# Moving splits, squares, sums and a state scan from GpSimd to VectorE, in a list-scheduled decoder layer

## The chip, the core and the metric

The kernel runs on one core of a Trainium2 chip. A core has TensorE (PE in the profile: matmuls, with PEld for its weight loads), VectorE (DVE), ScalarE (ACT), GpSimd (POOL) and SyncE (SP), which here issues the DMAs. Each engine runs its own instructions in order; semaphores tie the engines together. The metric is the time of one execution in microseconds, lower is better.

## The reference

One inference step of a one-layer hybrid decoder, in float32, for 512 prompt tokens and 64 sample tokens (8 sequences of 8). All branches read one input projection of the normed input:

```python
z = rmsnorm(x, norm_g) @ w_in          # 2048 -> 3904 columns, split into u, gates, cq, ckv, kr, qm
y_ssm = ssm_mixer(u, h0)               # 32 groups, 64 complex states: x_t = a * x_(t-1) + b u_t, GELU, GLU
y_mla = attend(q(cq), k(ckv, kr), v(ckv))   # 8 heads; the sample also attends to 1024 paged past tokens
y_mem = softmax(rmsnorm(qm) @ mk.T) @ mv    # 4 heads, 256 memory tokens
o = concat(rmsnorm(y_g) * silu(gate_g) for g in (ssm, mla, mem))
y = x + o @ w_out
```

The outputs are y for both kinds of tokens, the new latent rows, the memory's keys and values, and the last SSM states.

## The kernel before

Tokens lie along the free dimension (576 columns, done as two halves of 288), features along the 128 partitions. To keep float32 accuracy with the faster fp32r matmuls, every operand is split into two 12-bit parts: `hi` (a rounded copy, by ScalarE or VectorE) and `lo` (`tensor_tensor` subtract: what rounding left). A product is then three matmuls (`mm3`): hi by hi, hi by lo, lo by hi. So nearly each tile that TensorE reads has gone through one `hi` and one `lo`: weights (`wunit`, 512 columns), activations (`split`, 576 columns), softmax results.

The code doesn't issue instructions directly. `Hymba.record` writes them down in a sequential order, part by part: x (input and its squares), params (the SSM's discretised parameters, 16-wide steps), u, e (the SSM's input tables), q, kv, kr, qm (first projections), memkv, scan, memq and memh (memory attention), mla, ssm, glu, mems and samp (the sample's attention), gates, fin (norms of the branches) and out. Each recorded instruction has one or more forms: an engine with the time that `Eng.time` gives for it. `Plan.arrange` gives each a place and a due time from `ROWS`. `Plan.schedule` then is a list scheduler: it steps through time, and gives each free engine the ready instruction that is due first; an engine may take an instruction that is meant for another, if that other would be later by `self.steal` (0.2272 us). What comes out is one fixed order for each engine. `Plan.emit` issues it, so that nearly all instructions have line 603 of the kernel (transposes L602, memsets L600).

Before the change GpSimd is one of the engines in that game. `lo` (line 708) is meant for VectorE and may be taken by GpSimd; squares in `act` (733) are meant for ScalarE and may be taken by either; sums by `gtt` (803: sums of squares, rotary combinations) are meant for GpSimd and may be taken by VectorE. The scan over the states, `ssm_scan` (1084), is 248 instructions on GpSimd: for each of 7 steps inside groups of 8 chunks, 2 sample steps, 15 steps over groups and 7 steps that carry these back, it does eight products and sums, 256, 128, 16 and 240 columns wide, on the state tiles Z (named t_672 and t_690 in the order of before, t_650 and t_676 in the order of the change) and small tiles (F). The tables that `padded` makes (1002, part e and part ssm) and the memsets are on GpSimd too. In the scheduler's prices the engines don't disturb each other.

Of the kernel before, what the change touches and what calls it, by code (L numbers as in the profile page):

```python
# [11 lines left out]
F32R = mybir.dt.float32r  # L12
# [6 lines left out]
P = 128  # L19
NT = 576          # 512 prompt tokens, then 64 sample tokens (sequence, step)  # L20
# [4 lines left out]
SIZES = [74, 3170, 1400]         # SBUF: slots, columns for small float32 tiles and float32r ones  # L25
# [3 lines left out]
NC = 144          # chunks of 4 tokens  # L29
ZW = 153          # 1 + 128 prompt chunk states, 8 x 3 sample ones  # L30

# columns of the packed vectors
# [3 lines left out]
# the order of the program's parts: rows of streams that run side by side, each with its share of the row  # L36
# [17 lines left out]
# in_proj tiles  # L54
T_U, T_CQ, T_CKV, T_KR, T_QM, T_GS, T_GM, T_GMEM = 0, 4, 8, 10, 11, 15, 19, 27
# columns of the packed constants
# [3 lines left out]
def host_consts():  # L60
# [9 lines left out]
    # sums of all rows, of each 32 rows, of all rows eight times: a window of 40 columns puts them where they belong  # L70
# [93 lines left out]
class Tile_:  # L164
    """a piece of SBUF or PSUM, placed when the plan is made"""
# [9 lines left out]
class View:  # L175
    """an access pattern on a tile that has no place yet"""
# [62 lines left out]
def latency(a, b):  # L239
    """from the end of an engine's work to the start of another's that needs it"""  # L240
    if a == b:
        return (0.0, 0.127, 0.02, 0.102, 0.1)[a]
    return 0.26 if b == PE else 0.2 if a == PE else 0.15


FREED = (0.2, 0.15, 0.15, 0.15, 0.1)    # from the end of a tile's last use to its next use, in SBUF


# spaces: SBUF's slots of 576 columns; tiles with a place of their own; arenas for small float32 and float32r tiles; PSUM; DRAM
SLOT, OWN, SMALL, SMALLR, BANKS, DRAM = range(6)  # L250
PITCH = 4096        # of a row of a tile that has no place yet


class Plan:
    """Records the kernel's instructions in a sequential order, then issues them in one that keeps the engines busy."""

    def __init__(self, F, R, PS, sizes, place):
# [7 lines left out]
        self.soon = 21.0755                     # when work is due that the tensor engine doesn't wait for  # L265
        self.edf = True
        self.margin = [0, 0, 730, 0, 0]
        self.steal = 0.2272                     # how much later an engine must be for another to take its work
        self.look, self.stall, self.tol = 12, 120.4994, 5.0000
        self.late = False                    # work that may wait until it is needed  # L270
        self.slack = 1.0                     # how long work may wait that frees memory
        self.window = [43.3422, 40.6910, 40.6910, 40.6910, 40.0202]

# [1791 lines left out]
```

## Time and profile before

| what | value |
|---|---|
| median of 3 runs | 1306.81 us (1303.35 to 1307.94) |
| span of the profiled execution | 1303.6 us |
| PE busy | 1205.4 us (92%) |
| DVE busy | 933.3 us (72%) |
| ACT busy | 540.8 us (41%) |
| POOL busy | 543.3 us (42%), 703 instructions |
| mean granted TensorE clock | 0.963 |

The page gives no other time for the profiled execution than its span. "Busy" is the time in which an engine has an instruction in hand; an instruction that stands still in the middle counts as busy. The clock is the share of TensorE's full speed that was granted: 1.0 is 2.4 GHz, 0.5 is 1.2 GHz.

### The profile page before, as it was taken

To read this page: it belongs to the slowest core of one execution; us is meant where nothing else is said; L and a number is where in the kernel's file an instruction comes from. 1 tells how busy PE (TensorE), PEld (TensorE's weight loads), DVE (VectorE), ACT (ScalarE), POOL (GpSimd) and SP (SyncE) were. 2 spreads that over 40 slices of the span, in tenths; PEclk is the share of its full clock that TensorE was granted. 3 is DMA by queue.
4 is the path that set the end of the run, shared out by engine and by line. 5 is a ranking of instruction groups with operands and counts; after the bars stand their busy time and mean duration, and the time that the engine had idled before them with its cause. 6 is when DMAs were issued, how large, how long until landed. Compare 5 with 4: busy or idle time off the path is not lost. (4 is left out here: it accounts for less than half of the span.)

```text
span 1303.6 us, 24011 instructions
## 1 busy us (share of the span) xinstructions
PE 1205.4 (92%) x8428; PEld 1130.6 (87%) x8428; DVE 933.3 (72%) x2007; ACT 540.8 (41%) x1238; POOL 543.3 (42%) x703
## 2 busy tenths in 40 slices
PE   7889987978689989899999999999999997999998
PEld 7789977978578788789899999999999887999998
DVE  8996799946899798997885757475766899622210
ACT  7222322333486477775564434343333354212100
POOL 5575289989888677782230101000001345100000
PEclk8889998989799899989999999999999989999999
DMA  8243342132021245533543424333333465434310
GB/s 293 93 124 116 120 145 67 41 128 67 19 80 54 63 111 188 181 119 94 162 142 111 132 90 128 96 108 108 126 118 94 135 214 163 160 103 150 116 63 28
DMA packets 93324, 151.53 MB, mean 116 GB/s; under 512 B 10803, under 2 KB 36787, under 8 KB 93203
## 3 DMA queue, kind: packets, MB, share of 16 engines
q1 hardware_dynamic: 93202, 150.00, 36.6%
q8 instruction: 66, 1.08, 0.3%
q14 instruction: 56, 0.45, 0.1%
HBM read 129.87 MB, written 17.73 MB: 113 GB/s over the span
## 5 line engine op out<-in xcount | busy, mean ns | idle before, releaser
L603 PE MATMUL PS<-t,t 128*128 128x288 f32 (+7 forms) x7976 | 1162.8, 303 | 46.7 <-DVE t L603 26.0
L603 PEld LDWEIGHTS PS<-t,t 128*128 128x128 f32 (+2 forms) x7976 | 1087.8, 190 | 102.1 <-DVE t L603 28.1
L603 ACT ACTIVATE t<-t 128x512 fp32r<-128x512 f32 (+6 forms) x484 | 288.0, 614 | 393.6 <-DVE t L603 117.7
L603 DVE TENSOR_TENSOR t<-t,t 128x512 fp32r<-128x512 f32 (+6 forms) x412 | 330.0, 815 | 105.1 <-ACT t L603 52.3
L603 POOL TENSOR_TENSOR t<-t,t 128x512 fp32r<-128x512 f32 (+6 forms) x160 | 229.5, 1442 | 339.4 <-PE PS L603 105.3
L603 ACT ACTIVATE t<-PS 128x256 f32<-128x256 f32 (+6 forms) x316 | 124.7, 425 | 174.4 <-PE PS L603 149.3
L603 DVE TENSOR_TENSOR t<-PS,t 128x288 f32<-128x288 f32 (+5 forms) x226 | 89.9, 426 | 102.8 <-PE PS L603 96.5
L603 DVE TENSOR_REDUCE F<-t 128x4 f32<-128x512 f32 (+1 forms) x137 | 94.9, 705 | 68.2 <-ACT t L603 67.1
L603 POOL TENSOR_TENSOR F<-t,F 128x256 f32<-128x256 f32 (+3 forms) x157 | 106.2, 695 | 12.1 <-DVE F L603 5.7
L603 DVE SCALAR_TENSOR_TENSOR t<-t,F,t 128x576 fp32r<-128x576 f32 (+5 forms) x84 | 77.7, 939 | 10.2 <-DMA t<-re 9.5
L603 ACT ACTIVATE t<-t,F 128x576 fp32r<-128x576 f32 (+6 forms) x93 | 60.0, 664 | 29.8 <-DVE t L603 11.5
L603 DVE TENSOR_SCALAR t<-t 128x512 fp32r<-128x512 f32 (+6 forms) x109 | 53.2, 492 | 20.8 <-PE PS L603 5.7
L600 POOL MEMSET t<- 128x4 f32 (+3 forms) x86 | 31.2, 373 | 83.6 <-PE PS L603 36.6
L603 ACT COPY t<-PS 128x64 f32<-128x64 f32 (+7 forms) x135 | 38.0, 299 | 66.5 <-PE PS L603 61.3
L603 DVE SCALAR_TENSOR_TENSOR t<-t,t 128x576 f32<-128x576 f32 (+1 forms) x68 | 62.0, 923 | 2.1 <-ACT t L603 1.9
L603 PE MATMUL PS<-t,R 128*40 128x384 f32 (+6 forms) x134 | 31.3, 332 | 32.9 <-ACT t L603 16.5
L603 DVE SCALAR_TENSOR_TENSOR F<-F 128x64 f32<-128x64 f32 (+5 forms) x157 | 57.9, 374 | 1.8 <-POOL F L603 0.4
L603 PEld LDWEIGHTS PS<-t,R 128*40 128x40 f32 (+3 forms) x134 | 17.3, 146 | 39.2 <-ACT t L603 17.4
L603 POOL TENSOR_TENSOR t<-t,F 128x16 f32<-128x16 f32 (+4 forms) x64 | 45.8, 715 | 4.2
L603 POOL TENSOR_TENSOR F<-F 128x16 f32<-128x16 f32 (+4 forms) x66 | 41.3, 626 | 8.0 <-DVE F L603 3.7
L603 POOL TENSOR_TENSOR R<-F,R 64x64 fp32r<-64x64 f32 (+1 forms) x8 | 4.5, 561 | 78.8 <-DVE R L603 62.1
L603 DVE TENSOR_TENSOR F<-F 128x16 f32<-128x16 f32 (+4 forms) x125 | 33.7, 287 | 1.0
(76 smaller groups left out, 493.8 us busy)
## 6 DMA issues: line engine op xcount, KB each, us to landing
t<-in_w_in SPq DMA_DIRECT2D x124, 256.0 KB, 3.1
t<-in_w_out SPq DMA_DIRECT2D x64, 256.0 KB, 3.7
t<-in_pages SPq DMA_DIRECT2D x64, 224.0 KB, 2.8
t<-in_xT SPq DMA_DIRECT2D x48, 288.0 KB, 4.7
t<-re SPq DMA_DIRECT2D x32, 256.0 KB, 3.1
t<-in_pages SPq DMA_DIRECT2D x64, 128.0 KB, 2.1
re<-t SPq DMA_DIRECT2D x24, 256.0 KB, 2.5
out_yT<-t SPq DMA_DIRECT2D x16, 288.0 KB, 2.1
```

The lines of the kernel that those rows point to most:

```text
L600: return real(r["out"], r["value"])
L603: return real(**r)
```

## The change

1. Forms are taken away: `lo` has no GpSimd form, squares have none, and `gtt` is recorded for VectorE alone. The scan is recorded for VectorE.
2. The scheduler gets a resource, `port`. `Eng.shared` says which forms take it: on GpSimd each instruction with an SBUF input; on VectorE each with two SBUF inputs, and copies and tensor_scalar from SBUF to SBUF. Such a form is not started before `port`, and sets `port` to its end less 0.07 us.
3. TensorE's prices in `time` and `weights` rise: 2.23 instead of 2.4 columns a nanosecond for products, 2.35 for weights.

`ROWS`, the window, `steal` and all other settings stay. Comments are removed, which moves the lines (603 becomes 614). The core of the diff:

```diff
+        self.early = 0.07
...
+        port = 0.0
...
+                if e in (DVE, POOL) and port > now + 1e-9 and not h:
+                    continue
...
+                    if op.forms[e][2] and port > now + 1e-9:
+                        skipped.append(item)
+                        tries += 1
+                        why = "port"
+                        continue
...
+                    if op.forms[e][2]:
+                        port = op.end - self.early
...
-            nxt = [a for a in avail if a > now + 1e-9]
+            nxt = [a for a in avail + [port] if a > now + 1e-9]
...
-        return fn, self.time(name, kw)
+        return fn, self.time(name, kw), self.shared(name, kw)
+
+    def shared(self, name, kw):
+        src = [kw[k] for k in ("in_", "in0", "in1") if isinstance(kw.get(k), View)]
+        n = sum(v.t.space != BANKS for v in src)
+        if self.eng == POOL:
+            return n > 0
+        return self.eng == DVE and (n > 1 or n == 1 and name in ("tensor_copy", "tensor_scalar") and kw["out"].t.space != BANKS)
...
-            return 2 * kw["in_"].shape[0] / 2.4e3
-        return size(kw["lhsT"]) * (2 if kw["lhsT"].dtype == F32R else 4) / 2.4e3
+            return 2 * kw["in_"].shape[0] / 2.35e3
+        return size(kw["lhsT"]) * (2 if kw["lhsT"].dtype == F32R else 4) / 2.35e3
...
-                return 0.003 + 2 * kw["in_"].shape[0] / 2.4e3
+                return 0.003 + 2 * kw["in_"].shape[0] / 2.23e3
...
-            return (k if kw["lhsT"].dtype == F32R else 4 * max(k, 64)) / 2.4e3 + 0.003
+            return (k if kw["lhsT"].dtype == F32R else 4 * max(k, 64)) / 2.23e3 + 0.003
...
-            o = [] if self.onpsum(in_) or not self.flex else [(self.G, "tensor_tensor", kw)]
-            self.V.record("tensor_tensor", (), kw, o)
+            self.V.record("tensor_tensor", (), kw)
...
-            o += [(e, "tensor_tensor", k_) for e in (self.V, self.G)]
+            o.append((self.V, "tensor_tensor", k_))
...
-        kw = dict(out=out, in0=a, in1=b, op=op)
-        self.G.record("tensor_tensor", (), kw, [(self.V, "tensor_tensor", kw)] if self.flex else [])
+        self.V.record("tensor_tensor", (), dict(out=out, in0=a, in1=b, op=op))
...
-        self.ssm_scan(self.G)
+        self.ssm_scan(self.V)
```

GpSimd before, where the rotary key is split (part kr): the subtraction that fills t_2995 is the low part of the rotary key's tile, t_2953 and t_2973 are those of a weight unit and of a latent tile; the 16-wide rows are the scan.

```order
L603 TENSOR_TENSOR F<-t_672,F 128x16
L603 TENSOR_TENSOR F<-F 128x16
L603 TENSOR_TENSOR t_2953<-t_2896,t_2941 128x512
L603 TENSOR_TENSOR t_2973<-t_2528,t_2959 128x576
L603 TENSOR_TENSOR t_690<-t_690,F 128x16
L603 TENSOR_TENSOR t_2995<-t_2905,t_2983 128x576
```

VectorE in the changed order at the same place: t_2956 is now the rotary key's low part, t_2950 a latent tile's; the row with t_676 is the scan.

```order
L614 TENSOR_TENSOR t_2878<-t_2878,t_2429 128x576
L614 TENSOR_TENSOR t_2939<-t_2532,t_2903 128x576
L614 TENSOR_TENSOR t_2950<-t_2705,t_2915 128x576
L614 TENSOR_TENSOR t_2956<-t_2878,t_2944 128x576
L614 TENSOR_TENSOR R<-PS,R 64x256
L614 TENSOR_TENSOR t_2962<-t_2740,t_2775 128x512
L614 TENSOR_TENSOR t_2970<-t_2912,t_2952 128x512
L614 TENSOR_TENSOR t_2979<-t_2967 64x576
L614 TENSOR_TENSOR t_2991<-t_2941,t_2974 128x512
L614 TENSOR_TENSOR t_3002<-t_2967,t_2983 128x576
L614 TENSOR_TENSOR t_3010<-t_2979,t_2994 64x576
L614 TENSOR_TENSOR t_3020<-t_2959,t_3005 128x512
```

The split of the rotary key comes right behind the product that makes its tile (first row), and no scan instruction stands among these rows.

GpSimd before, where the first weight units of the attention (t_3565, t_3595, t_3615) are split: they stand behind the scan's last, 240-wide steps.

```order
L603 TENSOR_TENSOR F<-t_690,F 128x240
L603 TENSOR_TENSOR F<-F 128x240
L603 TENSOR_TENSOR t_672<-t_672,F 128x16x15
L603 TENSOR_TENSOR F<-t_690,F 128x240
L603 TENSOR_TENSOR F<-t_672,F 128x240
L603 TENSOR_TENSOR t_3565<-t_3469,t_3516 128x512
L600 MEMSET t_3585 128x512
L603 TENSOR_TENSOR t_3595<-t_3499,t_3563 128x512
L603 TENSOR_TENSOR t_3615<-t_3508,t_3593 128x512
```

VectorE in the changed order, where the same unit's low part (t_3608) is made:

```order
L614 TENSOR_TENSOR t_650<-t_650,F 128x16x15
L614 TENSOR_TENSOR t_3591<-t_1922,t_3446 128x576
L614 TENSOR_TENSOR t_3598<-t_2197,t_3485 128x576
L614 TENSOR_TENSOR F<-t_676,F 128x240
L614 TENSOR_TENSOR t_3608<-t_3487,t_3546 128x512
L614 TENSOR_TENSOR F<-t_650,F 128x240
L614 TENSOR_TENSOR t_3620<-t_2707,t_3254 128x512
```

Splits and scan now alternate on VectorE, one scan step between two splits.

GpSimd in the changed order, from the end of part e to the start of part ssm:

```order
L614 TENSOR_TENSOR F<-t_981,F 128x256 x2
L611 MEMSET t_1398 128x512
L614 TENSOR_TENSOR t_1398<-F 64x16x16 x2
L611 MEMSET R 64x2
L614 TENSOR_TENSOR t_688<-t_688 128x256
L611 MEMSET t_3394 128x512
L611 MEMSET t_3451 128x512
L614 COPY t_3451<-t_981 64x8x16 x2
```

Between the last table of e (t_1398) and the first memset of ssm (t_3394) two instructions are left, where the scan and the splits stood.

## Rows read from the trace of the kernel before

**Rows 1.** The page: part 1, busy time; the clock line of part 2.
```profile
PE 1205.4 (92%) x8428; PEld 1130.6 (87%) x8428; DVE 933.3 (72%) x2007; ACT 540.8 (41%) x1238; POOL 543.3 (42%) x703
...
PEclk8889998989799899989999999999999989999999
```
**Rows 2.** Stretches A to F: PE, PEld, DVE, ACT, POOL busy (count), clock, DMA.
```profile
0.00:161.00 161.00, 142.19 (x970) 136.64 (x971) 130.57 (x256) 60.66 (x118) 86.11 (x90) 0.94 0.47 151
161.00:337.00 176.00, 143.21 (x976) 137.53 (x974) 141.02 (x172) 52.85 (x92) 156.32 (x236) 0.90 0.26 83
337.00:568.00 231.00, 208.58 (x1624) 182.05 (x1622) 212.21 (x596) 158.27 (x407) 180.60 (x222) 0.97 0.35 105
568.00:1016.00 448.00, 442.73 (x2914) 409.67 (x2915) 311.59 (x750) 196.62 (x487) 69.83 (x114) 0.98 0.38 115
1016.00:1127.00 111.00, 96.23 (x656) 92.54 (x655) 98.48 (x164) 47.43 (x97) 50.48 (x43) 0.94 0.52 169
1127.00:1303.00 176.00, 172.43 (x1297) 172.20 (x1295) 39.43 (x73) 24.99 (x40) 0.00 (x0) 1.00 0.31 101
```
**Rows 3.** PE's largest wait: for whom; us in total, times, longest.
```profile
PE PS L603 <- DVE t L603: 36.4, 34, 4.4
```
**Rows 4.** Three holes of PE, as in rows 2.
```profile
217.00:223.00 6.00, 0.90 (x4) 0.90 (x5) 5.91 (x8) 1.15 (x2) 5.69 (x6) 0.51 0.00 0
267.00:274.00 7.00, 0.09 (x1) 0.09 (x1) 0.00 (x0) 0.00 (x0) 6.45 (x17) 0.84 0.40 136
322.00:334.00 12.00, 1.29 (x8) 1.08 (x7) 6.54 (x9) 3.65 (x6) 11.53 (x14) 0.68 0.00 1
```
**Rows 5.** Timeline of B: start, us, instruction [idle before it, released by].
```profile
212.91 5.51 DVE L603 SCALAR_TENSOR_TENSOR t<-t,F,t 128x576 f32<-128x576 f32 x4
...
222.10 2.26 PE L603 MATMUL PS<-t,t 128*128 128x288 f32 x8 [7.14 <-DVE F L603]
...
273.91 0.85 PE L603 MATMUL PS<-t,R 128*128 128x288 f32 x2 [6.92 <-POOL t L603]
...
326.26 2.24 ACT L603 ACTIVATE t<-t 128x512 fp32r<-128x512 f32 x4 [8.77 <-POOL t L603]
...
333.24 0.54 PE L603 MATMUL PS<-t,R 128*40 128x384 f32 x1 [10.71 <-ACT t L603]
```
**Rows 6.** Groups of VectorE by shape in F: busy, mean ns, idle before.
```profile
L603 DVE TENSOR_TENSOR t<-t,t 128x512 fp32r<-128x512 f32 x41 | 27.3, 688 | 42.4 <-ACT t L603 42.3
```
**Rows 7.** The same view, 0 to 600 us.
```profile
L603 DVE TENSOR_TENSOR t<-t,t 128x512 fp32r<-128x512 f32 x123 | 115.9, 952 | 26.9 <-PE PS L603 16.9 <-ACT t L603 7.9 <-POOL t L603 0.4
...
L603 DVE TENSOR_TENSOR t<-PS,t 128x512 fp32r<-128x512 f32 x24 | 16.3, 682 | 1.3 <-ACT t L603 0.8
L603 DVE SCALAR_TENSOR_TENSOR F<-F 128x16 f32<-128x16 f32 x27 | 15.8, 594 | 0.0
```
**Rows 8.** VectorE's timeline in A.
```profile
57.26 0.34 DVE L603 TENSOR_TENSOR F<-F 128x16 f32<-128x16 f32 x3
57.51 1.53 DVE L603 SCALAR_TENSOR_TENSOR t<-t,F,t 128x256 fp32r<-128x256 f32 x1
```
**Rows 9.** Groups of GpSimd over the whole span, columns as in rows 6.
```profile
L603 POOL TENSOR_TENSOR t<-t,t 128x512 fp32r<-128x512 f32 (+6 forms) x160 | 229.5, 1442 | 339.4 <-PE PS L603 105.3 <-DVE t L603 90.4 <-ACT t L603 70.9
L603 POOL TENSOR_TENSOR F<-t,F 128x256 f32<-128x256 f32 (+3 forms) x157 | 106.2, 695 | 12.1 <-DVE F L603 5.7 <-DVE t L603 1.4
L603 POOL TENSOR_TENSOR t<-t,F 128x16 f32<-128x16 f32 (+4 forms) x64 | 45.8, 715 | 4.2
L603 POOL TENSOR_TENSOR t<-F 64x256 f32<-64x256 f32 (+1 forms) x35 | 28.9, 826 | 1.9 <-DVE F L603 0.4
L603 POOL TENSOR_SCALAR t<-t 64x64 f32<-64x64 f32 (+4 forms) x24 | 20.5, 855 | 9.2 <-DVE t L603 7.0 <-DVE F L603 0.9
```
**Rows 10.** Timeline of E.
```profile
1066.99 1.95 DVE L603 TENSOR_TENSOR t<-t,t 128x576 fp32r<-128x576 f32 x1
...
1069.13 10.68 PE L603 MATMUL PS<-t,t 128*128 128x288 f32 x66 [2.60 <-DVE F L603]
```

More of the change, by code (lines that the diff above doesn't have):

```diff
@@ L1574, in fn @@
             return sp.dma_start(out=dst.real(), in_=pages[bass.ds(v, 1)].rearrange("o t d -> (o t) d")[:, c0:c1])
-        self.plan.add(SP, {SP: (fn, (c1 - c0) * P * 4.0)}, [dst], [pt], "page")
+        self.plan.add(SP, {SP: (fn, (c1 - c0) * P * 4.0, False)}, [dst], [pt], "page")
     def seq(self, b):
```

## Prediction

> **What bounds the kernel now.** Read the first part of the page first: PE is busy 1205.4 of 1303.6 us, and the clock line falls below 9 in single slices [rows 1]. PE is the bound, so only what makes PE wait can be won: 98.2 us of idle time, and what a slow clock takes. The busy time by stretch says where [rows 2]. I call the stretches A (0 to 161 us), B (to 337), C (to 568), D (to 1016), E (to 1127) and F. PE idles 18.8 us in A, 32.8 in B, 22.4 in C, 5.3 in D, 14.8 in E and 3.6 in F. D and F, nearly half of the time, have next to nothing to give. GpSimd is busy 423 of its 543 us in A to C and 50 in E, and those are the stretches in which PE waits.
>
> Who ends PE's waits? VectorE mostly [rows 3]. That doesn't yet blame GpSimd. So go to the three longest holes, all in B [rows 4]. From 267 to 274 us VectorE and ScalarE do nothing at all and GpSimd alone works; from 322 to 334 PE is busy 1.3 us and GpSimd 11.5 of 12. At 273.91 PE is released by GpSimd after 6.92 us [rows 5]: the split it needs (a "lo", 576 wide) stands on GpSimd behind the scan. At 326.26 ScalarE goes on after 8.77 us because a split was done on GpSimd, behind four scan instructions; PE follows at 333.24 after 10.71 us. At 222.10 PE waits 7.14 us for VectorE, which is busy throughout, at a slow pace: four 576-wide steps take 5.51 us.
>
> Why slow? Compare one shape where GpSimd rests (F) and in the first 600 us. The 512-wide subtraction of two SBUF tiles takes 688 ns in F and 952 ns on average before 600 us [rows 6, 7]. The same one with a PSUM input takes 682 ns there: no delay. The shortest suffer most: 16-wide steps average 594 ns, while three others of 16 columns together take 0.34 us [rows 7, 8]. A 256-wide step between them takes 1.53 us, twice the 512-wide one's time at rest [rows 8]. So a VectorE instruction with two SBUF inputs stands still while GpSimd reads SBUF, about as long as GpSimd's own instruction lasts (1442 ns on average for a split [rows 9]).
>
> **The change part by part.** Between the two orders 440 instructions leave GpSimd: 248 of the scan, 179 other tensor_tensor (mostly splits) and 13 squares. 427 go to VectorE, the squares to ScalarE but one. In addition some 135 instructions go from VectorE to ScalarE and 100 the other way, which I cost at nothing, since ScalarE is busy under 69% of every stretch [rows 2].
>
> GpSimd loses about 421 us of busy time: 229.5 + 106.2 + 45.8 us in the three large groups [rows 9], less some 24 of tables in the second, and some 64 in smaller ones, so that 543 becomes about 120. What stays are memsets and the padded tables of the SSM (28.9 + 20.5 us and the products before them) [rows 9].
>
> VectorE gains the work at its own price. The line through 688 ns at 512 columns and about 0.17 us at 16 is 0.15 us + 1.04 ns a column. The scan: 56 instructions of 256, 56 of 240, 16 of 128 and 120 of 16 columns give 23 + 22 + 5 + 20 = 70 us. The other moved work is about 110 us by the same line. Neighbours overlap by 0.08 us (three of 0.17 in 0.34), which takes 34 us off: 146 us in all, some 90 of it before 568 us. Against that stands the standing still that ends. From 123 subtractions 264 ns each, that is 32 us; with the 27 short steps (0.43 us each, 12 us) at least 44 us before 600 us [rows 7]; if all of VectorE's time in A to C shrank as the 512-wide one does (688 to 952), 134 of 484 us. So VectorE's A to C goes from 484 to between 440 and 530 us of 568 (484 + 90 less 134, or less 44). It carries more and is about as busy as before: that is what makes the change work or fail.
>
> Stretch by stretch, in time won.
> - B: GpSimd is nearly empty there in the new order (the second GpSimd excerpt). The hole at 274 goes (6.9): the split now stands ahead of the scan's short steps on VectorE, which was idle. Of the 7.1 at 222 I take 5: four 576-wide steps cost 5.51 instead of about 4 x 0.69 us, and splits around them the rest. Of the 10.7 at 333 I take 7: the split starts without the four scan instructions ahead of it, 4.5 us, and VectorE's own steps before and after stop stretching. That is 19 of 24.8. The clock: 0.90 in B is 17.6 us lost, some 8 of them inside the holes (0.49 x 6, 0.16 x 7 and 0.32 x 12, [rows 4]), so 9.7 outside; in proportion 7. B gives 26; bounds 12 (the hole at 274 and half of the next) and 42 (all idle time, and the clock's 9.7).
> - A: PE waits here for VectorE, whose short steps for the SSM parameters are stretched; but GpSimd still fills the padded tables there, so contention stays in part. 7 of 18.8 idle; bounds 0 and 18.
> - C: VectorE is busy 212 of 231 us. Six tenths of that, by my estimate from its shapes, read SBUF twice; shrunk by the ratio above (0.72), 212 becomes about 176; by the orders some 100 more instructions, of 0.4 us, bring it to 216. No room is won: 0; bounds -29 and +20.
> - D: 3, at its start, where GpSimd still splits (0 to 8). F: 0.
> - E: here GpSimd's splits stretch VectorE's norm steps (a 576-wide split at 1.95 us, after which PE waits 2.60, [rows 10]). All but small casts move: about 20 us more work on VectorE, against 50 us of GpSimd that no longer holds it up. Half of the 14.8 idle: 7 (0 to 14).
>
> The sum is 26 + 7 + 0 + 3 + 7 = 43 us: 1303.6 becomes 1260.6 by the profiled execution. Its span is 3.2 us under the median of the runs shown (1306.8), so the forecast is **1264 us**.
>
> The planner's new port rule also delays work: a VectorE step of two SBUF inputs is held until GpSimd's is done, by order alone, so nothing on chip waits that would not have stood still. I cost it at nothing; the cover is VectorE's PSUM-fed work, and without it the price is the rival below. The changed TensorE prices (7% longer) hardly move PE's order, which starts every part of the program within a few dozen of its 8418 instructions of where it stood, so PE's own work is the same.
>
> **The rivals.**
> *VectorE takes over (slower).* In C 216 us of its work and GpSimd's remaining 53 us (the tables for ssm) fall together. If each of these 53 us holds VectorE, C takes 269 instead of 231, 38 more; with the scan's steps ahead of splits in the same in-order queue, the other stretches give only half, 13 + 4 + 2 + 4 = 23. Net +15: 1322 us. It decides where VectorE's idle and held time in C exceeds some 38 us. For it: VectorE's 92% in C. Against it: some 90 of its 216 us there read PSUM or reduce, and the PSUM-fed 512-wide step shows no delay (682 ns).
> The Trainium skill, "SBUF — State Buffer", section Who interferes with whom, says that only instructions with two SBUF inputs or in a two-port mode meet GpSimd, and that the pair is locked for the whole instruction; by that rule C could hide the 53 us under the PSUM-fed work and the net would be the forecast; the 682 ns agrees.
> The Trainium skill, "Perfetto Trace Analysis", section Optimizing Scalar/DVE Operations, speaks against the change: where VectorE is saturated, offloading to ScalarE or even GpSimd may pay, though it adds that the shared port may undo that. By its first half C ends as in this rival.
>
> *The waits are dependences.* PE's waits end on chains (sum, norm, split) that pass PE, ScalarE and VectorE in turn; if only the hole at 274 and half of another were contention, 12 us are won: 1295 us. For it: VectorE and ScalarE release PE, not GpSimd [rows 3]. Against it: in the holes GpSimd is the engine at work [rows 4].
>
> *The small waits go too.* PE is "busy" in C while it waits in steps too short to count as idle. With A, B, D and E near their upper ends and half of C's: 14 + 36 + 6 + 12 + 20 = 88: 1219 us. For it: every stretched step sits in front of something. Against it: C's VectorE load.
>
> That the change doesn't do what it says is excluded by the orders, where GpSimd's part is down to about 260 instructions of 703.
>
> **How the numbers follow.** Forecast 0.60 (1243 to 1283), dependences 0.17 (1285 to 1304), small waits 0.13 (1205 to 1242), VectorE takes over 0.10 (1308 to 1335). The range leaves out the slower rival and the lower half of the best one: 1227 to 1302. A measurement here tells about 0.3% (4 us) from no change. Faster by more: 0.60 + 0.13 + 0.12 of the dependences = 0.85; within: 0.06; slower: 0.09.
>
> **What would show it.** Right: GpSimd's busy time near 120 us; the 512-wide subtraction before 600 us near 0.70 us instead of 0.95; none of the three holes of B left with GpSimd alone at work; B shorter by 20 us or more; E shorter by some 7; C unchanged; the clock line without the dips of B. VectorE's busy total stays near 930 us. Wrong: the holes of B in new places with VectorE busy on the scan (scan before splits), C longer with VectorE above 95%, or subtractions still near 0.9 us because the remaining GpSimd work meets them.

## The result, and the profile after

The changed kernel takes **1324.12 us** (median of 4 runs, 1321.45 to 1325.64), the kernel before on the same chip 1305.18 us (1303.35 to 1307.94). The ratio is **1.0131** (95% interval 1.0106 to 1.0156): slower by 17 us by the ratio, by 19 between the medians, where 1264 was forecast. The profiled execution has a span of 1319.7 us against 1303.6, so the two traces show 16 us of it.

The page of the changed kernel, part 1 and the clock line; then the stretches A to F, cut at the same of TensorE's instructions as before (columns as in [rows 2]: length, then PE, PEld, DVE, ACT, POOL busy with their counts, granted clock, DMA).

```profile
PE 1226.1 (93%) x8428; PEld 1144.2 (87%) x8428; DVE 940.4 (71%) x2400; ACT 567.7 (43%) x1285; POOL 131.3 (10%) x263
...
PEclk9999979998859778989989999989899997999999
```

```profile
0.00:140.00 140.00, 134.61 (x973) 131.15 (x973) 111.17 (x271) 67.81 (x131) 35.44 (x60) 0.99 0.54 176
140.00:296.00 156.00, 140.85 (x977) 134.98 (x975) 146.68 (x366) 61.70 (x107) 6.61 (x12) 0.93 0.29 92
296.00:574.00 278.00, 240.67 (x1622) 206.31 (x1622) 230.79 (x701) 165.66 (x425) 78.14 (x126) 0.83 0.27 83
574.00:1034.00 460.00, 445.00 (x2917) 410.47 (x2917) 319.19 (x793) 199.28 (x484) 11.07 (x65) 0.98 0.37 115
1034.00:1144.00 110.00, 93.00 (x652) 89.59 (x651) 93.32 (x201) 48.00 (x100) 0.00 (x0) 0.91 0.52 166
1144.00:1320.00 176.00, 171.93 (x1297) 171.70 (x1295) 39.30 (x72) 25.26 (x40) 0.00 (x0) 1.00 0.33 104
```

Compare with [rows 2]. A is 21 us shorter and B 20: by 296 us the changed kernel is 41 us ahead. C takes 278 us instead of 231 and D 460 instead of 448, which gives 59 us back; E is 1 shorter, F equal. In C the granted clock is 0.83 instead of 0.97 on average (it is 2.4 or 1.2 GHz at any time), and VectorE, now busy 231 us there instead of 212, is less full than before: 83% of the stretch instead of 92%.

The work moved as forecast. GpSimd is down to 131 us, and the standing still is nearly over: the 512-wide subtraction of [rows 7] took 952 ns on average and now takes about the 688 ns that it took at rest (groups of VectorE by shape, 0 to 600 us of the changed kernel: busy, mean ns, idle before):

```profile
L614 DVE TENSOR_TENSOR t<-t,t 128x512 fp32r<-128x512 f32 x181 | 123.0, 699 | 13.0 <-PE PS L614 9.7 <-ACT t L614 2.1
...
L614 DVE TENSOR_TENSOR F<-t,F 128x256 f32<-128x256 f32 x32 | 19.1, 624 | 0.3
...
L614 DVE TENSOR_TENSOR F<-t,F 128x240 f32<-128x240 f32 x28 | 16.3, 600 | 0.1
...
L614 DVE TENSOR_TENSOR t<-t,F 128x256 f32<-128x256 f32 x14 | 9.4, 670 | 0.2
...
L614 DVE TENSOR_TENSOR F<-F 128x256 f32<-128x256 f32 x15 | 6.4, 425 | 0.3
```

### The profile page after: what moved, and what is told of

Same layout as the page of the kernel before. It is cut to its first block, busy times and chain, and to the rows that moved or that the text cites. A ratio compares the mean times of both kernels' runs of the same rounds, so it can differ in the third digit from the quotient of the medians.

```text
span 1319.7 us, 23902 instructions
## 1 busy us (share of the span) xinstructions
PE 1226.1 (93%) x8428; PEld 1144.2 (87%) x8428; DVE 940.4 (71%) x2400; ACT 567.7 (43%) x1285; POOL 131.3 (10%) x263
## 4 chain that ended last, share of the span: by engine, by line
PE 73%; DVE 16%; ACT 3%; DMA 2%; issue 2%; SPq 1%; DVEq 0%; ACTq 0%
PE PS L614 71%; DVE t L614 10%; DVE F L614 5%; ACT t L614 3%; PE PS L613 2%; SPq L614 1%; DMA t<-in_pages 1%; ACT F L614 0%; DMA t<-re 0%; DMA t<-in_w_out 0%; DMA t<-in_w_in 0%; DMA t<-t 0%; DMA t<-in_rope 0%; DVE PS L614 0%; DVE R L614 0%
## 5 line engine op out<-in xcount | busy, mean ns | idle before, releaser
L614 PE MATMUL PS<-t,t 128*128 128x288 f32 (+6 forms) x7976 | 1171.5, 306 | 42.5 <-DVE t L614 19.6
L614 DVE TENSOR_TENSOR t<-t,t 128x512 fp32r<-128x512 f32 (+7 forms) x572 | 370.3, 666 | 99.9 <-ACT t L614 56.0
L614 ACT ACTIVATE t<-PS 128x256 f32<-128x256 f32 (+7 forms) x312 | 125.2, 425 | 192.8 <-PE PS L614 156.1
L614 DVE TENSOR_TENSOR t<-PS,t 128x288 f32<-128x288 f32 (+6 forms) x226 | 91.2, 429 | 105.6 <-PE PS L614 96.8
L614 DVE TENSOR_TENSOR F<-t,F 128x16 f32<-128x16 f32 (+3 forms) x128 | 45.9, 392 | 1.3
L614 DVE TENSOR_SCALAR t<-PS 128x512 fp32r<-128x512 f32 (+7 forms) x66 | 27.9, 437 | 23.9 <-PE PS L613 14.7
L614 DVE TENSOR_TENSOR F<-F 128x16 f32<-128x16 f32 (+6 forms) x186 | 42.0, 240 | 1.9
L614 PEld LDWEIGHTS PS<-t,R 128*40 128x40 f32 (+3 forms) x134 | 17.7, 149 | 23.2 <-DVE t L614 11.7
L613 PE MATMUL PS<-t,t 128*128 128x128 f32 (+2 forms) x152 | 30.1, 301 | 4.3 <-DVE F L614 1.9
L614 DVE SCALAR_TENSOR_TENSOR F<-F 128x64 f32<-128x64 f32 (+5 forms) x157 | 32.8, 218 | 1.4
L614 DVE TENSOR_TENSOR t<-t,F 128x16 f32<-128x16 f32 (+5 forms) x72 | 32.3, 449 | 1.3
```

Of the source, the lines that this page charges most:

```text
L613: return real(r["out"], r["in_"], r["identity"])
L614: return real(**r)
```

## The experiments

The change has three parts that can be had one by one: the moves off GpSimd, the port rule, and TensorE's new prices. All ratios are to the kernel before, run beside on the same chip; "C" is the stretch that holds the same of TensorE's instructions as 337 to 568 us of before.

### The parts apart

**Moves alone** (against the changed kernel; every 2.23e3 and 2.35e3 becomes 2.4e3):

```diff
-        return fn, self.time(name, kw), self.shared(name, kw)
+        return fn, self.time(name, kw), False
...
-        return size(kw["lhsT"]) * (2 if kw["lhsT"].dtype == F32R else 4) / 2.35e3
+        return size(kw["lhsT"]) * (2 if kw["lhsT"].dtype == F32R else 4) / 2.4e3
```

> The kernel before with the work moved off GpSimd and nothing else: the port is no resource and TensorE keeps its old prices. Load theory (VectorE, with 427 instructions more, is what makes 300 to 570 us long, in whatever order): 1315 to 1330 us, as with the whole change, and that stretch (TensorE instructions of 337 to 568 us of before) again about 278 us against 231. Order theory (the port rule or the new prices hand the work out in a worse order): 1262 to 1290 us, the stretch 225 to 240 us, the gains of 20 us each ahead of it kept. Fitted-settings theory (any redrawn order of this list loses, since its row shares and windows were fitted to the old one): 1310 to 1325 us, with the loss in other places than with the whole change.

Measured: 1301.20 us, ratio 0.9955 (0.9933 to 0.9977). No theory had that time: the gains ahead of C are there in full (A and B 300 us instead of 337), and C takes 260.

**Port rule alone** (before with the `port` lines of the change):

```diff
-        return fn, self.time(name, kw)
+        return fn, self.time(name, kw), self.shared(name, kw)
```

> The kernel before with the port rule alone: splits, sums and scan may still go to GpSimd, but none is handed out while the list's clock has the pair taken. Load theory: about as before, 1290 to 1310 us, since GpSimd still takes part. Order theory: 1320 to 1345 us, the loss in 300 to 570 us with TensorE thinly fed. Fitted-settings theory: 1310 to 1330 us.

Measured: 1365.24 us, ratio 1.0435 (1.0396 to 1.0474), more than any theory had. C takes 293 us, though VectorE's work there hardly grew (212 to 216): TensorE and VectorE both wait more.

**Prices alone** (before with 2.23e3 and 2.35e3):

```diff
-            return (k if kw["lhsT"].dtype == F32R else 4 * max(k, 64)) / 2.4e3 + 0.003
+            return (k if kw["lhsT"].dtype == F32R else 4 * max(k, 64)) / 2.23e3 + 0.003
```

> The kernel before with only TensorE's prices in the list changed (matrix columns at 2.23 instead of 2.4 a nanosecond, weights at 2.35): no instruction is moved by rule; 426 change their engine by the list's own choice. Load theory: 1300 to 1312 us, as before. Order theory with the port rule as cause: the same, 1300 to 1312 us; with the prices as cause: 1315 us or more, the loss in 300 to 570 us. Fitted-settings theory: 1312 to 1330 us, with TensorE waiting in new places.

Measured: 1333.62 us, ratio 1.0197 (1.0168 to 1.0226): four numbers in the list, and 27 us. That is the time of the order theory with the prices as cause, but not its place: A and B are 15 us longer, C only 11. And before redrawn by another setting comes to 1.0060 and 1.0234 (below), so this run alone doesn't show that it was the prices.

**The change without the port rule** (the first line pair of the first diff):

> The changed kernel without the port rule (moves and new prices stay). Load theory: 1318 to 1328 us, as the changed kernel. Order theory with the port rule as cause: 1262 to 1290 us, 300 to 570 us shorter by 35 us or more; with the prices as cause: 1318 to 1328 us. Fitted-settings theory: anywhere from 1300 to 1330 us, and not what the other three add up to.

Measured: 1312.39 us, ratio 1.0044 (1.0021 to 1.0067), a time that only the fitted-settings theory allowed. In this draw of the order the prices cost 0.9% on top of the moves (0.9955), and the rule 0.9% on top of these.

C of the four, in the order told, columns as above:

```profile
300.00:560.00 260.00, 227.54 (x1624) 196.08 (x1623) 229.30 (x695) 167.06 (x425) 82.98 (x126) 0.88 0.31 94
```

```profile
324.00:617.00 293.00, 244.33 (x1622) 208.04 (x1621) 216.35 (x572) 167.07 (x421) 206.86 (x272) 0.81 0.28 86
```

```profile
352.00:594.00 242.00, 218.13 (x1620) 189.86 (x1620) 210.22 (x608) 155.85 (x404) 166.06 (x209) 0.92 0.30 93
```

```profile
290.00:562.00 272.00, 233.64 (x1621) 201.80 (x1619) 233.50 (x706) 167.32 (x423) 83.31 (x128) 0.86 0.29 89
```

### VectorE's load in C

With the moves alone, the third column of C says 229 us of VectorE's work instead of 212. Following each instruction by its place in the two orders shows where that comes from (sums of single durations, which overlap a little; before against the moves alone; each instruction counts in the stretch in which it ran before; "own" are those that VectorE has in both):

| stretch | VectorE's own instructions, before | the same, moves alone | taken over from GpSimd | of it scan |
|---|---|---|---|---|
| A | 136.6 | 107.2 | 22.1 | 0 |
| B | 131.9 | 94.2 | 78.1 | 69.3 |
| C | 225.6 | 193.5 | 60.3 | 24.3 |
| D | 326.1 | 311.3 | 24.2 | 0 |
| E | 105.4 | 81.1 | 23.2 | 0 |

In C, besides, 53 instructions of VectorE (27 us) went to ScalarE and 41 (16 us) came from it. The end of the standing still pays for the new work in A and E, and not in B, C and D. B had 35 us of idle time on VectorE to take it, D 136; C had 19. Six runs follow that give VectorE less or other work in C, and one that gives C only work of TensorE.

**The scan stays on GpSimd** (against the moves alone):

```diff
-        self.ssm_scan(self.V)
+        self.ssm_scan(self.G)
```

> Moves alone (port no resource, old prices), but the scan stays on GpSimd: only splits, squares and sums leave it. The run with all moves alone took 260 us for the stretch C (TensorE's instructions that before ran from 337 to 569 us) against 232, after a gain of 37 us ahead of it; 24 to 30 us of VectorE's new work there was the scan. Load theory (C is as long as VectorE's work in it at about 90% busy): VectorE's work in C falls from 229 to about 205 us plus what GpSimd's scan holds up, C 230 to 245, and the gain ahead of C shrinks to about 25 us, since the scan meets VectorE's steps there again: 1282 to 1300 us. Order theory (in C the list hands work out badly, whoever does the scan): C 255 to 265 us, 1300 to 1315 us.

Measured: 1290.13 us, ratio 0.9891 (0.9860 to 0.9921). VectorE's work in C 212 us, C 241, B 169 instead of 156, since the scan is on GpSimd there again. These are the load theory's numbers. (50 instructions, 30 us, left VectorE in C; the others became 13 us longer.) Its C, columns as above:

```profile
313.00:554.00 241.00, 216.29 (x1626) 189.33 (x1624) 212.10 (x636) 164.36 (x425) 103.72 (x156) 0.93 0.34 103
```

**The scan alone moves** (before with that one line of the change):

> The scan alone goes to VectorE; splits, squares and sums may still go to GpSimd (port no resource, old prices). Load theory: GpSimd takes splits again, VectorE's work in C falls to 205 to 220 us, C 230 to 245 us; ahead of C part of the 37 us stays, because the two holes that the scan on GpSimd made are gone: 1280 to 1300 us. Order theory: C 255 us or more, 1300 to 1320 us.

Measured: 1327.59 us, ratio 1.0160 (1.0119 to 1.0202). Neither theory as put: I had expected VectorE's work in C to fall, but it rose to 239 us (the scan's steps, and splits still held up by GpSimd's 161 us there), and C to 267. The relation held, the estimate of the load didn't.

**GpSimd takes splits from C on** (against the moves alone, in `lo`):

```diff
-            self.V.record("tensor_tensor", (), kw)
+            o = [(self.G, "tensor_tensor", kw)] if self.plan.part in ('memq', 'memh', 'ssm', 'mla', 'mems', 'samp') and not self.onpsum(in_) else []
+            self.V.record("tensor_tensor", (), kw, o)
```

> All moves alone, but the low parts of the splits of the memory attention, the SSM output, the attention and the sample may go to GpSimd again; ahead of them GpSimd stays empty. The list then gives GpSimd 30 instead of 8 instructions of the attention, 19 more of the SSM output, 19 of the memory's sample and 47 of the sample. Load theory: the gain of 37 us ahead of C stays, VectorE's work in C falls from 229 to about 213 us as before the change, C 232 to 245 us, the holes of the stretch after it are as before the change or gone: 1268 to 1287 us, faster than both kernels. Order theory: C about 260 us again, 1295 to 1310 us. Contention theory (GpSimd's splits cost VectorE as much as they take off it): VectorE's work in C stays at 225 us or more, 1295 to 1310 us.

Measured: 1295.73 us, ratio 0.9918 (0.9882 to 0.9953). C only came to 252, with 226 us of VectorE's work: 52 of its instructions in C (33 us) went to GpSimd, which took 65 us for them, and those that both runs have on VectorE became 19 us longer. Both numbers are those of the contention theory. In part this is the redrawing: VectorE also took 54 instructions (25 us) over from ScalarE and gave it 38 (15 us). D came to 445 (below). The profiled execution, from which C and D are read, is the fastest of this kernel (1287.58 us).

**High parts on ScalarE** (against the moves alone, in `hi`):

```diff
-            o.append((self.V, "tensor_scalar", kw))
+            if self.plan.part not in ('memh', 'ssm', 'mla', 'mems'):
+                o.append((self.V, "tensor_scalar", kw))
```

> All moves alone, and the high parts in C for ScalarE alone; GpSimd gets nothing back. This takes load off VectorE in C (some 45 instructions, 13 us by the list's prices) without GpSimd. Load theory: C from 260 to 240 to 250 us, 1284 to 1295 us. Contention theory (C gets shorter only where GpSimd takes work): C stays 255 to 265 us, 1297 to 1306 us.

Measured: 1288.33 us, ratio 0.9870 (0.9829 to 0.9910), the load theory's time. VectorE's work in C 218, C 252: 8 us for 11 us of load, without GpSimd.

**The scan divided** (its last 56 instructions on GpSimd, the sample's splits free), and the same **with the high parts on ScalarE**:

```diff
-            step(zp[0][:, :, 1:, i], zp[1][:, :, 1:, i], qb(0, i, 15), qb(1, i, 15), zp[0][:, :, :15, 7], zp[1][:, :, :15, 7], [16, 15])
+            step(zp[0][:, :, 1:, i], zp[1][:, :, 1:, i], qb(0, i, 15), qb(1, i, 15), zp[0][:, :, :15, 7], zp[1][:, :, :15, 7], [16, 15], self.G)
```

> Moves alone, but with the scan divided: its first 192 steps on VectorE, the last 56 (240 columns wide, which fall into the stretch C) on GpSimd, and the sample's splits may go to GpSimd. Load theory (C is VectorE's work there, some 30 us on top, at a slope of 1.2 us per us as the runs so far lie): the gain of 33 to 37 us ahead of C stays, as in the run with all moves, C 238 to 248 us as with the scan on GpSimd, no TensorE holes of 5 to 10 us in the stretch after it, as in the run where the sample's splits could go to GpSimd: 1262 to 1280 us, faster than all so far. Order theory (what C takes has to do with the order drawn, not with VectorE's load): C 250 to 265 us, 1285 to 1305 us.

Measured: 1295.93 us, ratio 0.9933 (0.9903 to 0.9963): C 247 and D 445 as the load theory said, but B 174 instead of 156, so the time is not the load theory's.

> As the run with the divided scan, and the high parts of the splits of the memory attention, the SSM output and the attention are for ScalarE alone: some 40 of them leave VectorE in C, 14 us by the list's prices. Load theory: VectorE's work in C falls by 12 to 15 us more, C by 10 to 18 us: 1250 to 1270 us. If ScalarE takes over as the one that TensorE waits for (164 of 240 us in C so far), no gain or 5 us worse: 1262 to 1285 us.

Measured: 1289.37 us, ratio 0.9891 (0.9847 to 0.9936): VectorE's work in C 205, C 237, B 173 again. C is 10 us shorter for 12 us of load, as said; the time is longer than either theory's, by B.

**TensorE filled** (against the moves alone; 427 products of ones before 31 of TensorE's, two entries shown):

```diff
+FILL = {1990: 32, 1991: 3, ...}
...
+                for _ in range(FILL.get(k, 0)):
+                    w = min(P, size(o))
+                    self.nc.tensor.matmul(out=o.real()[:, :w], lhsT=self.ones.real()[:, :o.shape[0]], rhs=self.ones.real()[:, :w], start=True, stop=True)
```

> All moves alone, with 427 products of ones (128 columns, results overwritten at once) put in front of 31 of TensorE's products between 300 and 560 us, where the run with all moves alone showed TensorE late: they use about 25 us of the 65 us of lateness there. They change nothing but what TensorE does while it would wait. Clock theory (C is long because TensorE, thinly fed, falls to 1.2 GHz for 61 us there against 14 before, and then works slowly on the path): granted clock in C from 0.88 to 0.95 or more, C from 260 to 235 to 248 us, 1277 to 1290 us. Load theory: the clock rises but C stays 255 to 265 us, since VectorE sets it; 1297 to 1308 us. If the added products themselves delay what waits, C grows by up to 15 us.

Measured: 1336.01 us, ratio 1.0196 (1.0133 to 1.0258). C of this run, and the added products of full width, 384 of the 427 (groups of PE by shape):

```profile
296.00:591.00 295.00, 278.11 (x2056) 249.72 (x2055) 232.25 (x698) 169.11 (x426) 84.17 (x126) 0.88 0.27 83
```

```profile
L591 PE MATMUL PS<-R 128*128 128x128 f32 x384 | 52.9, 294 | 9.6 <-DVE t L622 5.4 <-ACT t L622 2.9 <-DVE F L622 1.2
```

They used twice the 25 us that I had set, the clock stayed at 0.88, and C grew by 35. So the run doesn't tell whether the slow clock makes C long or follows from it; that stays open. What it does say: 53 us more of TensorE's work in C, put where TensorE was late, cost 35 us of time though VectorE's work stayed nearly the same (232 us against 229). So C does not hang on VectorE alone.

### How much is the draw of the order?

Each setting of the scheduler gives one order, which I call a draw.

**The moves, redrawn.** `soon` says when work is due that TensorE doesn't wait for. Half a per cent of it changes next to no load (VectorE is busy 935 us in all instead of 937):

```diff
-        self.soon = 21.0755
+        self.soon = 21.2
```

> All moves alone, with one setting of the list moved by half a per cent (the time by which other engines' work is due, 21.0755 to 21.2): no work is moved by rule, but 109 instructions change their engine and 1814 of 8418 of TensorE's stand in another place. It shows how much a mere redrawing of the order is worth. If the order as such matters little: within 4 us of the run with all moves alone, 1297 to 1306 us, C 255 to 264 us. If any redrawing moves the time by as much as the port rule or the prices did: 1288 or less, or 1310 or more.

Measured: 1284.79 us, ratio 0.9843 (0.9800 to 0.9886): 1.1% from the first draw. So a difference of 10 us between two orders needs more than one draw of each. In C alone the draws of the moves lie 6 to 7 us apart (254 and 253 us after 260), so the 8 us of the two runs above that had C at 252 don't stand by themselves. The high parts on ScalarE have two more pairs of one setting: 10 us of C with the scan divided (247 to 237), and 9 at 21.2 (254 to 245, the last run below, where the sample's splits are free as well).

Hence the changed kernel redrawn, with and without the port rule, and before redrawn twice (20.9 and 20.0), the moves a third time (20.9), all by that one line.

> The changed kernel with the same setting moved from 21.0755 to 21.2 (79 instructions on another engine, 1359 of TensorE's 8418 in another place). If the port rule is what costs: 1312 to 1335 us again, and C at least VectorE's work plus 40 us (before the redrawing: 231 plus 47). If the changed kernel was merely a poor draw: 1285 to 1308 us, and C VectorE's work plus 25 to 35 us.

> The same without the port rule. If the rule costs: 10 to 25 us less than the redrawn changed kernel, C VectorE's work plus 25 to 38 us. If the rule costs nothing beyond the draw: within 8 us of it either way, or slower.

> The kernel before with that setting at 20.9 (278 instructions on another engine, 1543 of TensorE's in another place; at 21.2 the list finds no order that fits the memory). If the order of before is an unusually good draw: 1315 to 1335 us, and C is VectorE's work there plus 25 to 38 us instead of plus 18. If it is an ordinary one: 1298 to 1312 us, C plus 15 to 22 us.

> The kernel before with the setting at 20.0 (301 instructions on another engine than before, 1618 of TensorE's in another place; from the first redrawing it is as far). If the order of before is an unusually good draw: 1318 to 1340 us, C VectorE's work plus 25 to 38 us, the stretches A and B no shorter than before's. If the first redrawing was unusually bad: 1298 to 1312 us.

> All moves alone, the setting at 20.9, the third draw (the others took 1301 and 1285 us). If the moves gain on ordinary orders what they lose against the fitted one: 1282 to 1305 us, that is 25 to 45 us under the redrawn before. If the draw at 21.2 was merely lucky: 1305 to 1320 us.

Measured: the changed kernel 1.0153 (1.0115 to 1.0191), without the rule 1.0053 (1.0025 to 1.0081), before 1.0234 (1.0174 to 1.0294) and 1.0060 (1.0030 to 1.0089), the moves 0.9869 (0.9826 to 0.9911). C of the moves at 21.2, of the changed kernel redrawn, of that without the rule, and of before at 20.9:

```profile
293.00:547.00 254.00, 221.55 (x1617) 190.54 (x1616) 228.91 (x699) 167.52 (x427) 82.18 (x126) 0.91 0.31 95
```

```profile
296.00:570.00 274.00, 235.89 (x1628) 200.40 (x1628) 230.58 (x693) 168.14 (x428) 80.93 (x126) 0.86 0.28 86
```

```profile
290.00:568.00 278.00, 238.21 (x1624) 205.15 (x1623) 235.73 (x710) 167.27 (x424) 84.95 (x128) 0.84 0.29 87
```

```profile
344.00:594.00 250.00, 224.98 (x1623) 195.25 (x1622) 217.59 (x609) 157.32 (x405) 169.79 (x214) 0.90 0.32 95
```

The rule costs about as much again, but not in C, where the run without it is the longer one. The first redrawing of before came out as expected if the kernel before is a good draw, the second lies between the two answers. Together:

| order | draws, ratio to the kernel before | mean |
|---|---|---|
| before | 1, 1.0234, 1.0060 | 1.0098 |
| moves alone | 0.9955, 0.9843, 0.9869 | 0.9889 |
| moves and prices | 1.0044, 1.0053 | 1.0049 |
| moves, prices and port rule | 1.0131, 1.0153 | 1.0142 |

The groups of the last three rows don't touch; before's is 2.3% wide and takes in the last two. By the means the moves gain 2.1% (27 us) on a draw of before; the prices then cost 1.6% (21 us), the rule 0.9% (12 us). Draw by draw, the prices cost 0.9% in the first and 2.1% at 21.2, the rule 0.9% and 1.0%. And the kernel before is the best of its three draws, by 8 and 30 us, 13 under their mean: that much of what the change lost was this order's quality. With two or three draws each, the order of the last three rows is likely, and the sizes are rough.

### What the runs say of C

| run | C, us | VectorE busy in C | difference | clock in C |
|---|---|---|---|---|
| before | 231 | 212 | 19 | 0.97 |
| before redrawn (20.9; 20.0) | 250; 245 | 218; 218 | 32; 27 | 0.90; 0.91 |
| prices alone | 242 | 210 | 32 | 0.92 |
| moves alone, three draws | 260; 254; 253 | 229; 229; 229 | 31; 25; 24 | 0.88; 0.91; 0.91 |
| scan stays; scan alone | 241; 267 | 212; 239 | 29; 28 | 0.93; 0.90 |
| splits from C on; high parts on ScalarE | 252; 252 | 226; 218 | 26; 34 | 0.92; 0.88 |
| scan divided; with high parts | 247; 237 | 216; 205 | 31; 32 | 0.91; 0.94 |
| the last version below | 245 | 214 | 31 | 0.92 |
| moves and prices, two draws | 272; 278 | 234; 236 | 38; 42 | 0.86; 0.84 |
| the change, two draws | 278; 274 | 231; 231 | 47; 43 | 0.83; 0.86 |
| port rule alone | 293 | 216 | 77 | 0.81 |

C is VectorE's work there plus 24 to 34 us, in every order but three kinds: before's own (19), those with moves and new prices (38 to 47), and the port rule alone (77). (The run with TensorE filled is left out: 63.)

### A version that is faster than both

Moves alone at 21.2, high parts in C on ScalarE, the sample's splits free to go to GpSimd:

> All moves alone at 21.2, with the high parts in C for ScalarE alone and the sample's splits free to go to GpSimd. By the stretches of the runs so far: 142 ahead of B, B 150 to 156, C VectorE's 215 plus 25 to 35, that is 240 to 250, then 444 to 446 (no holes), 108 to 112 and 172: 1258 to 1280 us. If these gains don't add up (each was only a redrawing): 1280 to 1295 us.

Measured: 1278.94 us, ratio **0.9805** (0.9773 to 0.9836). That is within the first range. C is 245 and D 448; still it is only 6 us under the plain redrawing, no more than another draw can give.

## Why the prediction was wrong

That GpSimd's work held VectorE up was right, and five of the eight signs came. But the sum lacked what the scheduler's new numbers do, and it took the room in C as balanced, which it wasn't. Step by step:

**The scheduler's edits at nothing: the step that failed most.** I wrote of the port rule "I cost it at nothing", and of the prices that they "hardly move PE's order". By the means of the draws they cost some 33 of the 60 us between 1264 and 1324 (23 in the first draw, which is the changed kernel's own, 41 at 21.2). That nothing on the chip would wait that would not have stood still was wrong too: the rule alone, with splits still on GpSimd, cost 58 us. TensorE's order did change by a few places only (the prices alone: 4 on average, 90 at most), but that was the wrong measure: what counts is which work of TensorE stands between two steps that wait. One place in B shows it, the changed kernel against the one without the rule (timelines: start, us, instruction, idle before it and its releaser):

```profile
182.51 0.80 DVE L614 SCALAR_TENSOR_TENSOR t<-t,F,t 128x576 f32<-128x576 f32 x1
...
183.57 0.81 DVE L614 SCALAR_TENSOR_TENSOR t<-t,F,t 128x576 f32<-128x576 f32 x1
...
184.64 0.68 DVE L614 TENSOR_TENSOR t<-t,t 128x512 fp32r<-128x512 f32 x1
...
185.37 2.05 PE L614 MATMUL PS<-t,t 128*128 128x288 f32 x7 [7.73 <-DVE t L614]
```

```profile
173.75 8.51 PE L614 MATMUL PS<-t,t 128*128 128x288 f32 x53
...
183.17 0.68 DVE L614 TENSOR_TENSOR t<-t,t 128x512 fp32r<-128x512 f32 x1
...
183.91 1.86 PE L614 MATMUL PS<-t,t 128*128 128x256 f32 x13 [1.29 <-DVE t L614]
```

The split comes at about the same time. Without the rule TensorE has 53 products to do until then, with it none. Both draws with the rule have this hole (7.7 us) and B of 155 to 156 us; both without it, at the same prices, a wait of 1.0 to 1.3 us and B of 146. That is 9 of the rule's 12 us. But it isn't the rule's alone: the three draws of the moves at the old prices, without the rule, have it too (9.6 to 10.4 us) and B of 151 to 157. So the new prices had closed the hole, and the rule opened it again. TensorE with the moves alone, first draw:

```profile
187.89 2.50 PE L614 MATMUL PS<-t,t 128*128 128x512 f32 x5 [9.60 <-DVE t L614]
```

The prices' 21 us show as C longer by some 19 us and D by some 10, against B shorter by 9; why the new prices pack C worse is open.

**B: 26 forecast, 20 measured.** The holes at 273.91 and 333.24 [rows 5], where GpSimd worked alone, are gone; the clock in B only rose from 0.90 to 0.93. The 5 us at 222.10 were an error: I took VectorE to be late since it was slow. In the hole shown above, at about the same place of TensorE's order, it runs at full speed (0.80 us where 576-wide steps took 1.38 in [rows 5]), is busy throughout, and TensorE waits as long as before (7.73 against 7.14 us; 9.60 with the moves alone). The forecast's sign "holes in new places with VectorE busy" came true here, with norm steps and not the scan.

**A: 7 forecast, 21 measured,** above the bound of 18. I counted idle time alone; idle fell from 18.8 to 5.4 us, and the clock, 0.94 before and 0.99 now, gave the rest.

**C: 0 forecast, 47 lost,** the bound was 29. The claim that failed is "No room is won: 0": VectorE's work there was put at 216 us and is 229 with the moves alone. The term that was mis-sized is the new work, "some 100 more instructions, of 0.4 us": 99 came over from GpSimd and take 60 us (the table), 0.6 each. The scan's 240-wide steps that read Z cost 600 ns, not the 0.40 us of my line, which was read from splits (the rows of the profile after). The shrinking came nearly as put: 212 to 176 is 0.83, measured 0.86 (225.6 to 193.5). The exchange with ScalarE, costed at nothing, took 11 us off. Of the 47 us, 17 are this load, some 5 to 12 the loss of before's good order, and the rest, 18 to 25, came with the new prices; the rule's two pairs differ by +6 and -4 us in C.

**VectorE's total over A to C** was to lie between 440 and 530 us and is 489 (484 before). The sum was right and its place wrong: A got lighter by 19 us, C heavier by 19.

**The rival "VectorE takes over"** gave 1322 us, nearly the time that came, with C at 269. That is luck: A and B gave 41 us where it allowed 17, and C and D took 59 where it had 38 in C alone. Its mechanism is right in part only. C does follow VectorE's load; but GpSimd's remaining work (78 us in C, not the 53 assumed) isn't what held it, as the subtraction runs at 699 ns, and VectorE is 83% busy in C, not above 95%. The Trainium skill, "Perfetto Trace Analysis", section Optimizing Scalar/DVE Operations, says that work of a saturated VectorE may go to ScalarE or even GpSimd, and adds that between VectorE and GpSimd it might not help, since they share a port. The runs agree with both: in C the high parts on ScalarE gave 8 to 10 us in three pairs; the scan on GpSimd gave 19, of which B took 13 back, and splits on GpSimd gave 8, with VectorE's other steps 19 us longer.

**D: 3 forecast, 12 lost.** The three draws of the moves alone have 452 us in the mean, 4 more than before; the other 8 came with the new prices. The sample's attention is a chain of short steps, and its splits are now all VectorE's. In the changed kernel TensorE waits in the middle of it; in the fastest run, where these splits may go to GpSimd, other products stand there (timelines of PE):

```profile
677.92 0.30 PE L613 MATMUL PS<-t,F 128*64 128x128 f32 x1 [1.93 <-DVE F L614]
678.88 0.43 PE L614 MATMUL PS<-F,R 64*128 64x64 f32 x2 [0.66 <-DVE F L614]
681.67 0.58 PE L614 MATMUL PS<-R 64*128 64x258 f32 x1 [2.36 <-DVE R L614]
```

```profile
654.44 0.28 PE L613 MATMUL PS<-t,F 128*64 128x128 f32 x1
654.47 1.33 PE L614 MATMUL PS<-t,t 128*128 128x512 f32 x7
655.91 0.43 PE L614 MATMUL PS<-F,R 64*128 64x64 f32 x2
656.27 2.63 PE L614 MATMUL PS<-t,t 128*128 128x64 f32 x14
658.83 0.50 PE L614 MATMUL PS<-R 64*128 64x258 f32 x2
```

At the old prices and without the rule, D is 443 to 451 us where these splits may go to GpSimd and 448 to 458 where they may not; with all moves and the new prices it is 460 to 464, with the rule alone 461, with the prices alone 452.

**E: 7 forecast, 1 measured.** With the moves alone VectorE's own steps became 24 us shorter, but the work that it took over cost 23 (the table). In the changed kernel its busy time fell by 5 us only (98 to 93), and TensorE's waits moved to other places.

**Right were** GpSimd's 120 us (131), the subtraction near 0.70 us (0.699), VectorE's total near 930 us (940), the two holes of B, and F. On the mean of the draws the moves gain 27 us of the 43 forecast. The forecast compared them with one order, the best of three draws, and took that order's quality for granted.

## What to carry to other kernels

A change of a list scheduler's costs or rules is a change of every order: don't cost it at nothing because instructions move by a few places, and draw each order two or three times (move one harmless setting) before a difference of one per cent is put down to a cause. An engine's contention is weighed against the work it carries, stretch by stretch: moving work off a slow engine pays where the receiver has room (A, B), and costs where the receiver is nearly full (C), though hardly an instruction is held up any more. Where the receiver is full, give it less by another way: here the rounded copies on ScalarE shortened C in all three pairs. Leaving the scan on the slow engine shortened C too, but not the whole time beyond what a draw of the moves can give (1290 us against 1285 to 1301).

## What the runs showed of the hardware

The prediction had a VectorE step stand still about as long as GpSimd's own instruction lasts. On the whole GpSimd's work held VectorE up by much less: 108 us of it taken out of C made VectorE's own instructions there 32 us shorter, 150 us out of B 38, 50 out of A 29 (the table of VectorE's load, and the same instructions' time on GpSimd before). The mean of 952 ns hides two kinds: of these 123 subtractions 64 took under 0.72 us, and 45 over 1 us. It mostly depended on which engine was first. Over the whole trace of before, 26 subtractions of this shape began ahead of the GpSimd instruction that they overlapped, and 24 of them took under 0.72 us; 87 began while GpSimd had one with an input in hand, and only 20 of them did. Three steps that follow each other, in VectorE's and in GpSimd's timeline of before:

```profile
208.30 0.68 DVE L603 TENSOR_TENSOR t<-t,t 128x512 fp32r<-128x512 f32 x1
...
208.51 1.62 POOL L603 TENSOR_TENSOR t<-t,t 128x512 fp32r<-128x512 f32 x1 [0.74 <-DVE t L603]
...
208.90 1.78 DVE L603 TENSOR_TENSOR t<-t,t 128x512 fp32r<-128x512 f32 x1
```

The first runs at full speed into GpSimd's; the second starts while GpSimd's is under way and ends 0.55 us behind it. The Trainium skill, "SBUF — State Buffer", section Who interferes with whom, calls the pair of ports that the two engines share an exclusive lock; these rows agree. A scheduler that takes the pair as one resource prices every meeting in full: with splits still on GpSimd that cost 58 us.

A scan step that reads its state with a stride of eight elements, by a broadcast factor, takes 624 ns at 256 columns; one that reads and writes it so, without a broadcast, 670; one between small packed tiles 425 (the rows of the profile after).

In C, products added to TensorE where it was late cost 0.66 us of time for each us of theirs, and the granted clock stayed at 0.88 (one run).
